# Moving the turns' DRAM transfers and the bias tables from SyncE's queue to GpSimd's in a two-layer encoder

## The chip, the cores and the metric

The kernel runs on one core of a Trainium2 chip. The metric is the device time of one execution in microseconds (us); the kernel before took 889.69 us as the median of three runs (887.34 to 892.37). The engines are TensorE (PE, matrix products; PEld is its weight load), VectorE (DVE), ScalarE (ACT), GpSimd (POOL) and SyncE (SP). SyncE computes nothing here; it issues transfers between DRAM and on-chip memory, which run on 16 DMA engines.

## The reference, cut to what matters

Two residual layers over a sequence of 256 tokens of width 2048, then a final RMSNorm. All data is float32.

```python
def _layer_ab(x, ln, w_in, sink, w_out):
    hn = _rmsnorm(x, ln)
    aq, ak, av, bq, bk, bv, z = jnp.split(hn @ w_in, AB_SPLITS, axis=-1)
    ya = banded attention, 8 heads, 2 key heads, +-128 tokens, ALiBi, a sink per head
    yb = dilated mixture, 8 heads, ALiBi
    y = jnp.concatenate([ya, yb], axis=-1) * jax.nn.silu(z)
    return x + y @ w_out

def _layer_c(x, ln, w_in, rpb, w_out):
    hn = _rmsnorm(x, ln)
    cq, ck, cv, z = jnp.split(hn @ w_in, 4, axis=-1)
    y = neighbourhood attention, 16 heads, learned bias rpb
    return x + (y * jax.nn.silu(z)) @ w_out

def reference(...):
    x = _layer_ab(x, ...); x = _layer_c(x, ...)
    return _rmsnorm(x, ln_f)
```

## The kernel before

Each float32 operand is split into a high part and a rest, both of a type that TensorE multiplies at full rate, and each product is three matmuls (high x high, high x rest, rest x high). All weights come as 296 units of 128 x 1024 float32 (512 KB). One unit goes this way: SyncE loads it into one of five buffers `raw` (L136), ScalarE casts it to `wh` (L149), VectorE subtracts to `wl` (L150); `wh` and `wl` have three buffers each. TensorE then takes 12 matmuls of 512 columns for the unit (L205), or 24 of mixed sizes where a block makes one head (L172, L174).

`plan()` lists the blocks: the projections for values (`v`, `va`), keys (`ka`, `k`, in layer C `k4`), queries (`q`, `q4`), gates (`z`, four in each layer, 8 units each), then the output projections (`o`, `last`). In the text, layer A is the part with the first eight heads, layer B that with the second eight, layer C the second layer with 16 heads. Beside the blocks run the heads: scores on TensorE (L367 to L369), softmax on VectorE and ScalarE (L371 to L388), then a turn of the probabilities, their split (L407, L408) and the product with the values (L161 to L163). A counter of blocks (`tick`, `later`) says in which block each step of a head is written down; steps of gates stand in a list of chores that is worked off by one per unit.

A **turn** transposes a 256 x 256 tile. VectorE transposes 32 x 32 squares (L249), one transfer writes the tile to a DRAM buffer `bounce` (L251), and four transfers read it back, 32 partitions each (L258), into `pT`. A gate makes two turns. In layer C, queries and keys are turned as well, through DRAM buffers `pair` into `ka`. Each head also loads a table of biases, two transfers in layers A and B (L498), one in layer C (L503).

A gate's evacuation is four steps on ScalarE (L464, L465, for each half of the tokens) with steps of VectorE behind them (L466, then L249); it can start when TensorE has finished the block.

Every transfer before stands in SyncE's queue, in one order with the weight loads. Each engine works its instructions in order, and the order is not that of the source alone: when the program is built, a scheduler places the instructions of every engine by its own estimates of when their inputs are there. A change of queue can thus move instructions on other engines. The names end in numbers in the rows of that order (`wh_7434`), which are the same in both programs.

Of the kernel before, what the change touches and what calls it, by code (L numbers as in the profile page):

```python
# [25 lines left out]
B = 32  # L26
# [77 lines left out]
def build(tc, ctx, xt, xr_in, wt, head, sink, rpb, tabs, gl_in, out):  # L104
    nc = tc.nc
# [115 lines left out]
    def to_features(j):  # L221


        cols = [slice(c, c + S) for c in range(j * WO, (j + 1) * WO, S)]
        got = []

        def out_():
            got.extend(turn([xr[:, t, c] for t in range(NT)]) for c in cols)

        def in_():  # L230
            got[:] = [turned(b) for b in got]

        def parts_(i):
            src = got[i].rearrange("p a (c t i) -> p c t a i", c=NT, t=NT)
            for c in range(NT):
                k = cols[i].start // P + c
                h, lo = (xx[:, k, e].rearrange("p (t a i) -> p t a i", t=NT, a=NB) for e in range(2))
                nc.scalar.activation(h, src[:, c], AF.Copy, scale=g[:, 1, k:k + 1])
                for t in range(NT):
                    nc.vector.scalar_tensor_tensor(lo[:, t], src[:, c, t], g[:, 1, k:k + 1], h[:, t].bitcast(F32),  # L240
                                                   op0=OP.mult, op1=OP.subtract)

        return [out_, lambda: None, in_, lambda: None, lambda: parts_(0), lambda: parts_(1)]

    def turn(srcs, nm="bounce", n=3):

        tt = work.tile([P, NB, NT, NT, B], F32, name="tt")
        for t in range(NT):
            nc.vector.transpose(tt[:, :, :, t, :].rearrange("p b c i -> p c b i"), srcs[t])  # L249
        bounce = dram.tile([P, NB, NT * NT * B], F32, name=nm, bufs=n)  # L250
        nc.sync.dma_start(bounce, tt.rearrange("p b c t i -> p b (c t i)"))  # L251
        return bounce

    def turned(bounce, pool=work, nm="pT"):
        pT = pool.tile([P, NB, NT * NT * B], F32, name=nm)
        src = bounce.rearrange("(a j) b x -> b j a x", a=NB)
        for b in range(NB):
            nc.sync.dma_start(pT[b * B:(b + 1) * B], src[b])  # L258
        return pT

    R = {}
# [129 lines left out]
    def transposes(hh, p, v):  # L391

        bounce = turn([p[:, t, :] for t in range(NT)])
        later(1, lambda: back(hh, bounce, v))

    def back(hh, bounce, v):
        pT = turned(bounce)
        later(L2, lambda: parts(hh, pT, v))
# [58 lines left out]
    def gate(pss, j):  # L457
# [13 lines left out]
        def out_(i):  # L471
            got[i] = turn([zr[:, i * S:(i + 1) * S] for zr in zs])

        def in_(i):
            got[i] = turned(got[i])
# [17 lines left out]
    def table_ab(hh):  # L493
        tab = work.tile([P, NT, S], F32, name="tab", bufs=2)
        n = 2 * S - 1
        for t in range(NT):
            src = bass.AP(tensor=tabs.tensor, offset=tabs.offset + hh * n + t * P, ap=[[1, P], [1, S]])
            nc.sync.dma_start(tab[:, t, :], src)  # L498
        return tab

    def table_c(hh):
        tab = work.tile([P, NT, S], F32, name="tab", bufs=2)
        nc.sync.dma_start(tab, rpb[hh])  # L503
        return tab

    def load_x(k0, k1):
# [36 lines left out]
    def start_head(lag, idx, q):  # L543
        if idx < AQ:
            k, v, sc = KA[idx // 4], (lambda: V["a"], idx // 4), (nsk[:, idx:idx + 1], sk[:, idx:idx + 1])
        else:
            vb = V["b"]
            k, v, sc = cur["k"], (lambda: vb, idx % 4), None
        tab = table_ab(idx)
        later(lag, lambda: scores(idx, q, k, v, tab, sc, -1))  # L550
# [16 lines left out]
    def start_pair(lag, j, i, bq, bk):  # L567

        got, tabs_ = {}, []

        def in_():
            for nm, b in (("k", bk), ("q", bq)):
                got[nm] = turned(b[i], qk, "ka")
            tabs_.append(table_c(j))

        def parts_():
            for nm in "kq":
                src = got[nm].rearrange("p a (c t i) -> p c t a i", c=NT, t=NT)
                got[nm] = []
                for c in range(NT):  # L580
                    h = qk.tile([P, S], F32R, name=nm + "h", bufs=3 if nm == "q" else 2)
                    lo = qk.tile([P, S], F32R, name=nm + "l", bufs=3 if nm == "q" else 2)
                    hv, lv = (e.rearrange("p (t a i) -> p t a i", t=NT, a=NB) for e in (h, lo))
                    nc.scalar.copy(hv, src[:, c])
                    nc.vector.tensor_sub(lv, src[:, c], hv.bitcast(F32))
                    got[nm].append((h, lo))

        def score(i):
            v = (lambda: V[j // 4], j % 4 + i)
            scores(j + i, got["q"][i], got["k"][i], v, tabs_[i], None, 1)  # L590

        later(lag, in_)
        later(lag + 1, parts_)
        later(lag + 2, lambda: score(0))
        later(lag + 3, lambda: tabs_.append(table_c(j + 1)))
        later(lag + 2 + PACE, lambda: score(1))
# [132 lines left out]
```

## Time and profile before

| | before |
|---|---|
| median of three runs | 889.69 us |
| profiled execution, time | 889.07 us |
| profiled execution, span | 887.3 us |
| TensorE busy | 868.3 us (98%) |
| VectorE busy | 599.0 us (68%) |
| ScalarE busy | 502.4 us (57%) |
| GpSimd busy | 0.9 us |
| SyncE's DMA queue, share of 16 engines | 71.7% |

Busy time leaves out the issue of transfers, so SyncE has no row here. Matmuls overlap in the records: one of 512 columns shows a span of 0.39 us, and the next starts 0.227 us after it.

### The profile page before, as it was taken

The page shows a single profiled execution, that of the slowest core. Times are in us where ns is not written, and L with a number is a line of the kernel's source. Part 1 is how long each engine was busy: PE and PEld are TensorE (multiplying, and loading weights), DVE is VectorE, ACT ScalarE, POOL GpSimd, SP SyncE. Part 2 cuts the span into 40 slices and gives each one's busy share as a digit, 9 for nine tenths or more (in the row PEclk, how much of TensorE's full clock was granted, in tenths as well). Part 3 has the DMA queues.
Part 4 walks back from the last instruction along what each step waited for, and adds up shares of the span by engine and source line. Part 5 has one row for each costly group of instructions (what it writes and reads, how often), then busy time and mean ns, then how long its engine had stood idle before and what let it go on. Part 6 is the DMA issues. An engine that isn't in the chain of part 4 may idle for free.

```text
span 887.3 us, 12303 instructions
## 1 busy us (share of the span) xinstructions
PE 868.3 (98%) x4218; PEld 732.9 (83%) x4218; DVE 599.0 (68%) x972; ACT 502.4 (57%) x858; POOL 0.9 (0%) x7
## 2 busy tenths in 40 slices
PE   9999999999999999999999999999999998899995
PEld 7898888889888888888888888888888876688884
DVE  6576867788677766667556666766666666666563
ACT  7646666676556555555455565556555655454452
POOL 0000000000000000000000000000000000000000
PEclk9999999999999999999999999999999999999999
DMA  9868777779767677777677767786687578667642
GB/s 353 305 201 256 223 248 254 214 228 278 225 211 233 230 239 252 245 240 241 214 238 233 258 223 259 226 268 243 200 272 272 196 220 297 197 208 274 210 165 96
DMA packets 104607, 209.53 MB, mean 236 GB/s; under 512 B 11744, under 2 KB 52704, under 8 KB 104416
## 3 DMA queue, kind: packets, MB, share of 16 engines
q1 hardware_dynamic: 104544, 208.74, 71.7%
q8 instruction: 33, 0.54, 0.3%
q14 instruction: 30, 0.25, 0.1%
HBM read 187.72 MB, written 20.97 MB: 235 GB/s over the span
## 4 chain that ended last, share of the span: by engine, by line
PE 94%; ACT 2%; DVE 1%; DMA 1%; issue 1%; SPq 0%; ACTq 0%; DVEq 0%
PE pp L205 70%; PE pp L172 10%; PE pp L174 6%; PE pp L293 1%; PE pp L292 1%; PE pp L294 1%; PE pS L369 1%; PE pY L163 1%; PE pY L162 1%; PE pS L368 1%; PE pS L367 1%; PE pY L161 1%; DMA raw<-wt 1%; DMA y<-xt 1%; PE pp L176 1%; ACT wh L149 1%
## 5 line engine op out<-in xcount | busy, mean ns | idle before, releaser
L150 DVE TENSOR_TENSOR wl<-raw,wh 128x1024 fp32r<-128x1024 f32 x291 | 354.5, 1222 | 218.7 <-ACT wh L149 188.8
L205 PE MATMUL pp<-wh,xx 128*128 128x512 f32 (+1 forms) x1472 | 457.1, 387 | 6.3 <-ACT wh L149 6.0
L149 ACT CAST wh<-raw 128x1024 fp32r<-128x1024 f32 x291 | 305.0, 1052 | 255.2 <-PE pp L205 207.1
L205 PEld LDWEIGHTS pp<-wh,xx 128*128 128x128 f32 x1472 | 275.8, 189 | 62.0 <-ACT wh L149 7.0
L205 PE MATMUL pp<-wl,xx 128*128 128x512 f32 (+1 forms) x736 | 285.3, 388 | 2.7 <-DVE wl L150 2.7
L205 PEld LDWEIGHTS pp<-wl,xx 128*128 128x128 f32 x736 | 139.4, 189 | 31.3 <-DVE wl L150 4.9
L205 PE MATMUL pp<-wh,yy 128*128 128x512 f32 x448 | 138.4, 389 | 0.0
L205 PEld LDWEIGHTS pp<-wh,yy 128*128 128x128 f32 x448 | 84.1, 188 | 17.5
L172 PE MATMUL pp<-xx,wh 128*128 128x512 f32 x390 | 93.7, 392 | 0.0
L205 PE MATMUL pp<-wl,yy 128*128 128x512 f32 x224 | 87.1, 389 | 0.0
L172 PEld LDWEIGHTS pp<-xx,wh 128*128 128x128 f32 x390 | 72.1, 188 | 14.6
L174 PEld LDWEIGHTS pp<-xx,wl 128*128 128x128 f32 x416 | 53.3, 191 | 2.0
L174 PE MATMUL pp<-xx,wl 128*128 128x256 f32 x416 | 54.0, 283 | 0.0
L205 PEld LDWEIGHTS pp<-wl,yy 128*128 128x128 f32 x224 | 42.1, 188 | 8.6
L379 ACT ACTIVATE s<-s,nm 128x256 f32<-128x256 f32 x64 | 32.0, 501 | 12.1 <-DVE nm L374 10.2
L371 DVE SCALAR_TENSOR_TENSOR s<-pS,qs,tab 128x256 f32<-128x256 f32 x64 | 28.4, 475 | 5.1 <-PE pS L369 5.0
L249 DVE STREAM_TRANSPOSE tt<-p 128x256 f32<-128x256 f32 x64 | 26.2, 435 | 7.9 <-ACT p L388 7.9
L388 ACT ACTIVATE p<-s,rd 128x256 f32<-128x256 f32 x64 | 29.0, 501 | 4.3 <-DVE rd L385 4.2
L181 ACT COPY sum<-pp 128x256 f32<-128x256 f32 x26 | 9.6, 371 | 37.5 <-PE pp L176 37.4
L407 ACT CAST ph<-pT 128x256 fp32r<-128x256 f32 x64 | 23.3, 405 | 11.3 <-DMA pT<-bounce 11.3
L408 DVE TENSOR_TENSOR pl<-pT,ph 128x256 fp32r<-128x256 f32 x64 | 24.4, 418 | 6.1 <-ACT ph L407 6.0
L374 DVE TENSOR_REDUCE nm<-s 128x2 f32<-128x512 f32 x32 | 21.7, 679 | 0.2
(124 smaller groups left out, 582.5 us busy)
## 6 DMA issues: line engine op xcount, KB each, us to landing
raw<-wt SPq DMA_DIRECT2D x295, 512.0 KB, 4.5
bounce<-tt SPq DMA_DIRECT2D x56, 256.0 KB, 2.7
pT<-bounce SPq DMA_DIRECT2D x224, 64.0 KB, 3.3
tab<-tabs SPq DMA_DIRECT2D x32, 128.0 KB, 4.9
tab<-rpb SPq DMA_DIRECT2D x16, 256.0 KB, 4.1
pair<-tt SPq DMA_DIRECT2D x16, 256.0 KB, 3.0
ka<-pair SPq DMA_DIRECT2D x64, 64.0 KB, 4.0
xr<-xr SPq DMA_DIRECT2D x4, 512.0 KB, 5.2
```

Of the source, the lines that this page charges most:

```text
L149: nc.scalar.copy(h, raw)
L150: nc.vector.tensor_sub(lo, raw, h.bitcast(F32))
L172: nc.tensor.matmul(ps, parts[u][0][:, c], aa[:, k], start=k == 0, stop=False)
L174: nc.tensor.matmul(ps[:, 0], parts[u][1][:, c], aa[:, k, 0], start=False, stop=False)
L205: nc.tensor.matmul(pss[t], aa[:, k, i // 2, t * P:(t + 1) * P], (h, lo, h)[i][:, c], start=k == 0 and i == 0, stop=k == NK - 1 and i == 2)
L249: nc.vector.transpose(tt[:, :, :, t, :].rearrange("p b c i -> p c b i"), srcs[t])
L371: nc.vector.scalar_tensor_tensor(s[:, t, :], pS[:, t, :], R["qs"][:, t:t + 1], tab[:, t, :], op0=OP.mult, op1=OP.add)
L374: nc.vector.tensor_reduce(nm, s, axis=AX.X, op=OP.max, negate=True)
L379: nc.scalar.activation(s[:, t, :], s[:, t, :], AF.Exp, bias=nm[:, t:t + 1], accum_out=den[:, t:t + 1])
L388: nc.scalar.activation(p[:, t, ::step], s[:, t, :], AF.Copy, scale=rd[:, t:t + 1])
L407: nc.scalar.copy(dh, src)
L408: nc.vector.tensor_sub(dl, src, dh.bitcast(F32))
```

## The change

Four places are edited, and in each `nc.sync` becomes `nc.gpsimd`: the write of a turn, its four reads, and the two kinds of bias table. The loads of weights, of the input and of the residual, and the output, stay in SyncE's queue.

```diff
@@ turn
-        nc.sync.dma_start(bounce, tt.rearrange("p b c t i -> p b (c t i)"))
+        nc.gpsimd.dma_start(bounce, tt.rearrange("p b c t i -> p b (c t i)"))
@@ turned
         for b in range(NB):
-            nc.sync.dma_start(pT[b * B:(b + 1) * B], src[b])
+            nc.gpsimd.dma_start(pT[b * B:(b + 1) * B], src[b])
@@ table_ab
-            nc.sync.dma_start(tab[:, t, :], src)
+            nc.gpsimd.dma_start(tab[:, t, :], src)
@@ table_c
-        nc.sync.dma_start(tab, rpb[hh])
+        nc.gpsimd.dma_start(tab, rpb[hh])
```

SyncE, at the first two gates of layer C, before: `raw` are weight loads, `ka` and `pT` reads of turns, `bounce` writes.

```order
L136 DMA raw_7104<-wt 128x1024
L136 DMA raw_7122<-wt 128x1024
L258 DMA ka_7163<-pair_6722 32x4x128 x4
L258 DMA ka_7168<-pair_6495 32x4x128
L251 DMA bounce_7161<-tt_7158 128x512
L258 DMA ka_7168<-pair_6495 32x4x128 x3
L503 DMA tab_7173<-rpb 128x512
L136 DMA raw_7177<-wt 128x1024
L251 DMA bounce_7186<-tt_7183 128x512
L136 DMA raw_7200<-wt 128x1024
```

SyncE at the same place after:

```order
L136 DMA raw_7104<-wt 128x1024
L136 DMA raw_7122<-wt 128x1024
L136 DMA raw_7177<-wt 128x1024
L136 DMA raw_7200<-wt 128x1024
L136 DMA raw_7244<-wt 128x1024
```

Only weight loads are left. GpSimd's queue at this place after:

```order
L251 DMA bounce_7161<-tt_7158 128x512
L251 DMA bounce_7186<-tt_7183 128x512
L258 DMA pT_7223<-bounce_7161 32x4x128 x2
L251 DMA bounce_7209<-tt_7206 128x512
L258 DMA pT_7223<-bounce_7161 32x4x128 x2
L258 DMA pT_7250<-bounce_7186 32x4x128 x4
L258 DMA pT_7273<-bounce_7209 32x4x128 x4
L251 DMA bounce_7375<-tt_7372 128x512
L258 DMA pT_7425<-bounce_7375 32x4x128 x4
```

Writes and reads of turns follow one another there in one order, as they did on SyncE, without weight loads between them.

ScalarE at the end of the second gate of layer C (`pp_7175` and `pp_7176` hold the block), before. `wh_7399` is the last unit of this block, `wh_7434` the first of the next:

```order
L149 CAST wh_7399<-raw_7267 128x1024
L454 CAST yy_88<-y_87 128x256 x2
L464 ACTIVATE s_7415<-pp_7175,rh_4422 128x512
L465 ACTIVATE sq_7416<-pp_7175,rh_4422 128x512
L464 ACTIVATE s_7420<-pp_7176,rh_4422 128x512
L465 ACTIVATE sq_7421<-pp_7176,rh_4422 128x512
L149 CAST wh_7434<-raw_7316 128x1024
L149 CAST wh_7457<-raw_7340 128x1024
```

ScalarE at the same place after:

```order
L149 CAST wh_7399<-raw_7267 128x1024
L379 ACTIVATE s_7297,den_7308<-s_7297,nm_7306 128x256 x2
L454 CAST yy_88<-y_87 128x256 x2
L388 ACTIVATE p_7313<-s_7297,rd_7311 128x256 x2
L454 CAST yy_88<-y_87 128x256
L423 COPY y_87<-pY_7364 128x256
L454 CAST yy_88<-y_87 128x256
L149 CAST wh_7434<-raw_7316 128x1024
L149 CAST wh_7457<-raw_7340 128x1024
L464 ACTIVATE s_7415<-pp_7175,rh_4422 128x512
L465 ACTIVATE sq_7416<-pp_7175,rh_4422 128x512
L464 ACTIVATE s_7420<-pp_7176,rh_4422 128x512
```

The casts of the next block's first two units have moved from behind the gate's evacuation to before it. VectorE's subtractions for these units move in the same way, and so does the third gate of layer C (`pp_7430`). At the other six gates two casts of the next block stand before the evacuation in both programs.

## Rows read from the trace of the kernel before

**Rows 1.** The page: busy time of the engines, chain that ended last.

```profile
PE 868.3 (98%) x4218; PEld 732.9 (83%) x4218; DVE 599.0 (68%) x972; ACT 502.4 (57%) x858; POOL 0.9 (0%) x7
...
PE 94%; ACT 2%; DVE 1%; DMA 1%; issue 1%; SPq 0%; ACTq 0%; DVEq 0%
```

**Rows 2.** TensorE by stretch (from:to, length, busy, count, granted clock, DMA share, GB/s).

```profile
60.00:700.00 640.00, 640.00 (x3155) 1.00 0.74 240
700.00:740.00 40.00, 35.02 (x161) 1.00 0.67 222
740.00:775.00 35.00, 31.36 (x129) 0.90 0.69 225
```

**Rows 3.** Timeline of TensorE, 725 to 790 us: start, length, operation, [idle before <-releaser].

```profile
737.58 0.73 PE L205 MATMUL pp<-wh,xx 128*128 128x512 f32 x2 [2.77 <-ACT wh L149]
739.16 0.50 PE L205 MATMUL pp<-wl,xx 128*128 128x512 f32 x1 [0.85 <-DVE wl L150]
...
765.88 0.73 PE L205 MATMUL pp<-wh,xx 128*128 128x512 f32 x2 [2.77 <-ACT wh L149]
767.48 0.80 PE L205 MATMUL pp<-wl,xx 128*128 128x512 f32 x1 [0.87 <-DVE wl L150]
```

**Rows 4.** TensorE in short stretches behind the two pairs, columns as in rows 2.

```profile
740.00:744.00 4.00, 4.00 (x12) 0.57 0.99 330
768.00:772.00 4.00, 4.00 (x13) 0.66 0.79 243
```

**Rows 5.** Timeline of ScalarE around the second and the fourth gate's evacuation.

```profile
734.17 0.69 ACT L464 ACTIVATE s<-pp,rh 128x512 f32<-128x512 f32 x1 [0.87 <-PE pp L205]
...
736.47 2.95 ACT L149 CAST wh<-raw 128x1024 fp32r<-128x1024 f32 x3
...
788.72 1.05 ACT L149 CAST wh<-raw 128x1024 fp32r<-128x1024 f32 x1 [0.51 <-ACT wh L149]
790.71 0.69 ACT L464 ACTIVATE s<-pp,rh 128x512 f32<-128x512 f32 x1 [0.94 <-PE pp L205]
```

**Rows 6.** SyncE's issues from 695 us, its longest wait there, ScalarE's wait behind it.

```profile
699.02 2.32 SPq L258 DMA_DIRECT2D ka<-pair  x5
...
712.60 0.38 SPq L136 DMA_DIRECT2D raw<-wt  x1
...
SPq L251 <- DVE tt L249: 7.4, 1, 7.4
...
717.18 1.05 ACT L149 CAST wh<-raw 128x1024 fp32r<-128x1024 f32 x1 [2.89 <-DMA raw<-wt]
```

**Rows 7.** DMA issues (count, KB, us to landing); SyncE's time per issue, ns min/median/max.

```profile
bounce<-tt SPq DMA_DIRECT2D x56, 256.0 KB, 2.7
pT<-bounce SPq DMA_DIRECT2D x224, 64.0 KB, 3.3
...
L258 SPq DMA_DIRECT2D pT<-bounce x224: 302/424/1863, 73.4 to 802.1; - x112
L251 SPq DMA_DIRECT2D bounce<-tt x56: 319/327/456, 70.7 to 795.5; - x56
```

**Rows 8.** The page's groups: the transposes of a turn (busy us, mean ns | idle before).

```profile
L249 DVE STREAM_TRANSPOSE tt<-p 128x256 f32<-128x256 f32 x64 | 26.2, 435 | 7.9 <-ACT p L388 7.9
```

**Rows 9.** Chain in order of time (start, length): the periods of layers A and C.

```profile
69.62 16.35 PE pp L205 x72
...
105.51 16.35 PE pp L205 x72
...
488.37 5.47 PE pp L205 x24
...
506.17 5.47 PE pp L205 x24
```

**Rows 10.** ScalarE's waits from 60 to 310 us: total, times, longest.

```profile
ACT ph L407 <- DMA pT<-bounce: 9.9, 4, 3.4
```

**Rows 11.** VectorE's costliest group, columns as in rows 8.

```profile
L150 DVE TENSOR_TENSOR wl<-raw,wh 128x1024 fp32r<-128x1024 f32 x291 | 354.5, 1222 | 218.7 <-ACT wh L149 188.8 <-issue 8.7 <-PE pp L174 6.1
```

## The prediction, made before the changed kernel ran

> **What bounds the kernel now.** I read the page's busy times and chain first. TensorE is busy for 868.3 of 887.3 us, and matmuls make up 94% of the chain that ended last [rows 1]. VectorE, ScalarE and the DMA engines have room. A change can thus only win what TensorE loses, so the next view is its busy time by stretch [rows 2]: nothing lost in the 640 us from 60 to 700, 4.98 us (40 - 35.02) from 700 to 740, 3.64 us (35 - 31.36) from 740 to 775. The rest lies at the head and the tail, which the change doesn't reach. The timeline of TensorE [rows 3] shows where in that stretch: two pairs of gaps, 2.77 + 0.85 us at 737 and 2.77 + 0.87 us at 765, together **7.26 us**; the other 1.4 us are four gaps under 0.5 us from 714 to 732. After each pair the granted clock falls, though TensorE is busy again: over 4 us it averages 0.57 after the first and 0.66 after the second [rows 4], a stretch at the lower of its two levels (1.2 GHz) and the rest at the upper (2.4 GHz). What that costs is the share not granted: 4 x 0.43 + 4 x 0.34 = **3.1 us**.
>
> Why there? The rows of ScalarE [rows 5] show it. At 734.17 ScalarE starts a gate's evacuation (L464), which had to wait until TensorE finished the gate's block, and only behind the four evacuation steps comes the next cast of weights, at 736.47; VectorE's half follows. TensorE has nothing split in advance, so it stands still. The third gate's pair at 765 has the same releasers and sizes [rows 3]. At the fourth gate, casts (the last at 788.72) stand ahead of the evacuation at 790.71, and TensorE has no gap there. It is an order on two engines, fixed when the program is built: I counted the weight units cast ahead of each gate's evacuation beyond that gate's own block. Of the eight gates six have two units ahead, and the second and third gate of layer C have none.
>
> SyncE's queue shows the rest [rows 6]: from 699.02 to 712.60 no weight load is issued, because a turn's write (L251) waits 7.4 us for its transposes and the loads stand behind it. ScalarE then waits for weights, 2.89 us before 717.18, and the four small gaps lie about and after that.
>
> **What the change does, step by step.** It moves 408 transfers from SyncE to GpSimd, counted in the order of the changed program: 72 writes (56 to `bounce`, 16 to `pair`), 288 reads back (four for each) and 48 bias tables. SyncE loses 72 x 0.33 + 288 x 0.42 = 145 us of issuing [rows 7], and the tables'; it is not on the path, so that alone is worth nothing. What counts is what stood behind them: weight loads now wait only for one of their five buffers. The 13.6 us hole can't recur, and I take the 1.4 us of small gaps as gone.
>
> The larger part comes with the build. The order of the changed program has two units of the next block ahead of all eight gates, on ScalarE and on VectorE alike, the two bad ones included (wh_7434 and wh_7457 now stand before the evacuation of pp_7175). That is the place of the six good gates, and TensorE lost nothing at those. So both pairs go, with the clock after them: 7.26 + 3.1 = **10.3 us** (10.34).
>
> Against this stands a longer turn. GpSimd's price p of a transfer isn't in this trace; it is busy for 0.9 us in all [rows 1]. Bounds from the nearest rows: SyncE's issue of the same transfers, 0.33 to 0.42 us, below, and the longest that any of them took there, 1.86 us, above [rows 7]. Below the lower bound nothing would change, since even at SyncE's price the sum doesn't hang on p. I take 0.4 to 1.2 us, nearer the medians than the one longest row, and work out where p begins to matter.
>
> *Latency.* A turn writes (2.7 us to landing), then issues four reads in a row, the last landing 3.3 us after its issue [rows 7]: 2.7 + (p - 0.33) + 3p + 3.3 + (p - 0.42) = 5.25 + 5p, which is 7.4 us at SyncE's price. In the changed order the tightest turns have three weight units between transposes and first use (15 of the 56 turns that pass through `bounce`; 28 have four, 13 five). In layer C a unit takes 17.8 / 6 = 2.97 us [rows 9]. ScalarE casts unit k when TensorE frees the buffer of unit k-3, so transposes end 1.05 (a cast, [rows 5]) + 1.22 (a subtraction, [rows 11]) + 2 x 0.435 [rows 8] = 3.1 us after one such point, and the first use stands 1.05 us after a point three units later: 3 x 2.97 + 1.05 - 3.1 = 6.8 us are free. Beyond that ScalarE waits, and TensorE's split units cover 3 x 2.97 - 1.05 - 0.87 - 2.27 = 4.7 us of it (the cast before, two casts of pT, taken like the transposes of that tile, and cast and subtraction of the next unit). That such waits are covered the trace shows: from 60 to 310 us ScalarE waits up to 3.4 us for pT [rows 10], and TensorE is never idle there [rows 2]. So a turn costs nothing until 5.25 + 5p exceeds 6.8 + 4.7 = 11.5, **p = 1.25**.
>
> *Throughput.* A waiting transfer holds all behind it on GpSimd, so each write-to-read wait (2.7 us) counts as use. Layer A, per gate and two heads: 24 transfers and three waits in 35.9 us [rows 9], full at p = 27.8 / 24 = 1.16. Layer B, per head: 7 and one in four units, 11.9 us at C's pace, 1.31. Layer C, per head: 11 and one in 17.8 us, 1.37. The second gate of C: 21 and two in about 24 us (96 matmuls at 16.35 / 72 = 0.227 us are 21.8, and heads), 0.89; there a backlog of 21p + 5.4 - 24 forms, 3.6 us at p = 1.06, which the cover above absorbs. So up to p near 1.2 the sum is the same.
>
> The page "DMA: Bandwidth & Descriptors" of the Trainium skill (section "Latency and other measured facts") gives about 0.6 us to the first byte from SyncE's kind of queue and about 1 us from GpSimd's. By that, as an estimate, p would be 0.42 + 0.4 = 0.8 us and the sum unchanged; no run here shows it yet.
>
> At the start one table load now stands on GpSimd ahead of its copy of the gains (L532); that copy has to wait for the first input transfer, and the load lies beside this wait.
>
> **Sum.** 889.07 - 10.3 = 878.8; the 1.4 us of small gaps go, and I put the same amount back for turns that come late at the crowded second gate. The profiled execution lies 0.6 us below the median of the three runs; I say **879.0 us**, 1.2% faster.
>
> **Rivals.** *GpSimd's queue becomes the bound.* From about p = 1.25 on it is slower. At p = 1.3 layer A is over by 24 x 1.3 + 8.1 - 35.9 = 3.4 us, three times; C's second gate by 8.7, the two gates after it by 15 x 1.3 + 5.4 - 24 = 0.9 each; late turns add some 1: 878.8 + 22 = 901 us. What could make p so large is VectorE holding up the writing of descriptors. Its rows [rows 11] are 291 subtractions with two operands in SBUF of 1.22 us, 354.5 us of busy time; were a transfer held for one of them, p would be 0.43 + 1.22 = 1.65 and the time 878.8 + 131 = 1010 us (A 35, B 19, C 49, gates 28). Against it: such a subtraction is under way 40% of the time, so a transfer would wait 0.4 x 0.6 = 0.25 us on average, p = 0.7. The page "SBUF — State Buffer" of the Trainium skill (section "Who interferes with whom") speaks against this change: the writing of GpSimd's transfers starves while VectorE runs in a mode that takes both ports, which copies and tensor_scalar can enter but tensor_tensor has no such mode. By that rule these subtractions leave it alone, and the sum stands.
>
> *The gaps are paid back.* Weight loads start as soon as a buffer is free and meet the turns on the same 16 engines; in stretches these are already full (share 0.99 from 740 to 744) [rows 4]. With p around 1.2 and landings of 4 to 8 us instead of 3.3, the 15 tight turns leave TensorE short by 0.5 us each, with a dip of the clock: 878.8 + 10 = 889 us, no change. For it: that DMA share. Against: 640 us at a mean share of 0.74 without a gap [rows 2].
>
> *The change doesn't do what it says.* Were lateness of weights not behind anything, the time would stay at 889. But six good gates against two bad ones speak for the order, which the build has changed.
>
> **How the numbers follow.** Forecast (876 to 885 us) 0.65; paid back or without effect (885 to 894) 0.14; GpSimd as the bound (894 to 1010) 0.21. Half a per cent, 4.4 us, is about what a measurement of this kernel can tell from no change, so these are also the chances of faster, same and slower. The low end, 876 us, has the 1.4 us gone as well and 1 us of noise; to leave out no more than 2 in 10, the high end goes to p = 1.28, 898 us.
>
> **What would show it.** Right: no gap over 0.5 us on TensorE from 730 to 775, clock 1.00 there, no ScalarE wait for raw, about 878 us; ScalarE's waits for pT longer than 3.4 us in places, with TensorE busy. Right on p: GpSimd's transfers start 0.4 to 1.2 us apart. Wrong: starts over 1.25 us apart with reads queued behind reads, ScalarE waiting for pT at most heads, TensorE idle from about 70 us on (layer A first), the clock at 0.50 again and again.

## The result, and the profile after

| | before | after |
|---|---|---|
| median | 889.34 us | **940.11 us** (936.38 to 946.85) |
| ratio | | 1.058, 95% interval 1.053 to 1.062 |
| profiled execution, span | 887.3 us | 937.4 us |
| mean granted clock of TensorE | 0.994 | 0.982 |
| TensorE idle before its last matmul, in gaps over 0.1 us | 10.0 us, 10 gaps | 41.6 us, 37 gaps |

The changed kernel is 5.8% slower. The medians in this table come from runs side by side on one chip. The forecast was 879 us and the range ended at 898, so the time lies far outside it. (The gaps were added up from the timeline of TensorE; the first of each column is the 1.05 us ahead of the first matmul.) The median before is over six executions, one of which took 4205 us; without it the median is 888.99 us.

The page of the changed kernel: busy times, as in [rows 1], and its DMA issues (count, KB each, median us from issue to landing), as in [rows 7].

```profile
PE 887.5 (95%) x4218; PEld 739.3 (79%) x4218; DVE 595.3 (64%) x972; ACT 498.6 (53%) x858; POOL 224.4 (24%) x415
...
raw<-wt SPq DMA_DIRECT2D x295, 512.0 KB, 4.4
bounce<-tt POOLq DMA_DIRECT2D x56, 256.0 KB, 3.2
pT<-bounce POOLq DMA_DIRECT2D x224, 64.0 KB, 4.7
```

Reads that took 3.3 us to land now take 4.7; writes take 3.2 instead of 2.7. GpSimd is busy for a quarter of the span, so issuing doesn't fill its time.

The waits of the changed kernel (engine, line, what it waited for: total us, times, longest us):

```profile
ACT wh L149 <- PE pp L205: 144.9, 92, 3.8
ACT ph L407 <- DMA pT<-bounce: 133.1, 30, 8.8
...
DVE pl L408 <- ACT ph L407: 106.0, 27, 8.0
...
PE pp L205 <- ACT wh L149: 18.3, 10, 3.5
...
PE pp L205 <- DVE wl L150: 14.0, 16, 2.1
```

The second row is the new one. Before, ScalarE waited for `pT` 7 times, 11.3 us in all and 3.4 at most; now it waits 30 times, 133.1 us in all and up to 8.8. ScalarE works in order, so the next casts of weights stand behind such a wait, and the last two rows are TensorE's waits for those casts and for VectorE's half.

TensorE by stretch, columns as in [rows 2] with every engine's count:

```profile
60.00:700.00 640.00, 612.91 (x2964) 512.20 (x2964) 413.01 (x681) 342.02 (x603) 171.47 (x313) 0.99 0.71 224
700.00:740.00 40.00, 35.09 (x156) 28.19 (x155) 23.70 (x38) 21.57 (x40) 16.28 (x30) 0.96 0.77 235
740.00:775.00 35.00, 35.00 (x167) 29.41 (x166) 22.34 (x34) 18.71 (x32) 9.45 (x18) 1.00 0.69 229
```

From 60 to 700 us, where TensorE lost nothing before [rows 2], it is now idle for 640 - 612.9 = 27.1 us. In the changed kernel's stretch from 740 to 775 it is full.

One of the turns, 318 to 338 us. The timelines of the engines (start, length, engine, line, operation, [idle before <-releaser]), merged by start:

```profile
318.16 0.41 ACT L407 CAST ph<-pT 128x256 fp32r<-128x256 f32 x1 [4.46 <-DMA pT<-bounce]
...
320.86 1.05 ACT L149 CAST wh<-raw 128x1024 fp32r<-128x1024 f32 x1
...
320.96 16.67 SPq L136 DMA_DIRECT2D raw<-wt  x5
...
321.82 0.42 DVE L249 STREAM_TRANSPOSE tt<-p 128x256 f32<-128x256 f32 x1
...
322.24 1.05 ACT L149 CAST wh<-raw 128x1024 fp32r<-128x1024 f32 x1
...
322.54 0.56 POOL L251 DMA_DIRECT2D bounce<-tt  x1 [8.20 <-DVE tt L249]
...
323.80 1.05 ACT L149 CAST wh<-raw 128x1024 fp32r<-128x1024 f32 x1 [0.50 <-PE pp L205]
...
326.74 2.19 POOL L258 DMA_DIRECT2D pT<-bounce  x4 [3.64 <-issue]
...
332.55 0.41 ACT L407 CAST ph<-pT 128x256 fp32r<-128x256 f32 x1 [7.43 <-DMA pT<-bounce]
...
336.08 0.49 PE L205 MATMUL pp<-wh,xx 128*128 128x512 f32 x1 [2.69 <-ACT wh L149]
337.34 0.79 PE L205 MATMUL pp<-wl,xx 128*128 128x512 f32 x1 [0.77 <-DVE wl L150]
```

The first row is the end of the previous turn's wait. This turn's transposes end at 322.24, its write goes out at 322.54, the four reads from 326.74 to 328.93, and ScalarE can go on at 332.55, 10.0 us after the write. It waited 7.43 us; TensorE lived on its split units for 4.0 of them and then stood still for 2.69 + 0.77 us. All the while SyncE issued weight loads, five from 320.96 on. In the kernel before, at the next turn of the same part of the program, SyncE's own timeline reads:

```profile
305.73 0.33 SPq L251 DMA_DIRECT2D bounce<-tt  x1
307.46 0.33 SPq L136 DMA_DIRECT2D raw<-wt  x1
307.88 1.80 SPq L258 DMA_DIRECT2D pT<-bounce  x4
309.78 7.24 SPq L136 DMA_DIRECT2D raw<-wt  x4
```

One weight load goes out between write and reads, and the next four only after the reads.

### The profile page after: what moved, and what is told of

Same layout as the page of the kernel before. It is cut to its first block, busy times and chain, and to the rows that moved or that the text cites. A ratio compares the mean times of both kernels' runs of the same rounds, so it can differ in the third digit from the quotient of the medians.

```text
span 937.4 us, 12426 instructions
## 1 busy us (share of the span) xinstructions
PE 887.5 (95%) x4218; PEld 739.3 (79%) x4218; DVE 595.3 (64%) x972; ACT 498.6 (53%) x858; POOL 224.4 (24%) x415
## 5 line engine op out<-in xcount | busy, mean ns | idle before, releaser
L205 PE MATMUL pp<-wh,xx 128*128 128x512 f32 (+1 forms) x1472 | 466.1, 393 | 20.2 <-ACT wh L149 17.6
L149 ACT CAST wh<-raw 128x1024 fp32r<-128x1024 f32 x291 | 300.9, 1049 | 161.2 <-PE pp L205 144.9
L205 PEld LDWEIGHTS pp<-wh,xx 128*128 128x128 f32 x1472 | 280.4, 192 | 80.9 <-ACT wh L149 21.6
L205 PE MATMUL pp<-wl,xx 128*128 128x512 f32 (+1 forms) x736 | 290.6, 395 | 13.3 <-DVE wl L150 13.3
L205 PEld LDWEIGHTS pp<-wl,xx 128*128 128x128 f32 x736 | 141.4, 192 | 46.0 <-DVE wl L150 19.4
L258 POOL DMA_DIRECT2D pT<-bounce x224 | 122.4, 554 | 131.9 <-DMA bounce<-tt 69.7
L407 ACT CAST ph<-pT 128x256 fp32r<-128x256 f32 x64 | 23.3, 404 | 133.1 <-DMA pT<-bounce 133.1
L251 POOL DMA_DIRECT2D bounce<-tt x56 | 31.2, 558 | 242.2 <-DVE tt L249 231.1
L172 PEld LDWEIGHTS pp<-xx,wh 128*128 128x128 f32 x390 | 72.1, 188 | 14.8 <-ACT wh L149 0.4
L498 POOL DMA_DIRECT2D tab<-tabs x32 | 17.6, 555 | 104.4 <-DVE s L371 103.9
L258 POOL DMA_DIRECT2D ka<-pair x64 | 34.9, 551 | 30.3 <-DMA pair<-tt 13.1
```

What stands on the lines that cost most here:

```text
L149: nc.scalar.copy(h, raw)
L172: nc.tensor.matmul(ps, parts[u][0][:, c], aa[:, k], start=k == 0, stop=False)
L205: nc.tensor.matmul(pss[t], aa[:, k, i // 2, t * P:(t + 1) * P], (h, lo, h)[i][:, c], start=k == 0 and i == 0, stop=k == NK - 1 and i == 2)
L251: nc.gpsimd.dma_start(bounce, tt.rearrange("p b c t i -> p b (c t i)"))
L258: nc.gpsimd.dma_start(pT[b * B:(b + 1) * B], src[b])
L407: nc.scalar.copy(dh, src)
```

## The experiments

Two theories. **Theory 1:** transfers that GpSimd issues are slow by themselves (their landing, or GpSimd's price for each). **Theory 2:** whose queue it is doesn't matter; what matters is that weights and turns stood in one queue. There the waits for transposes and for a write's landing held the weight loads back too, so a turn's reads met few of them on the DMA engines. In two queues the weights run on beside the turns. Two side causes were open too: the tighter order that the build made, and the tables at the start. (The texts on record call the second theory Rival 2 in the swap and Theory 2 from the light weights on; under later use, Theory 1 means late turns in a tight order.)

All the runs in one table. "In flight" is the mean number of weight loads issued and not landed when a read is issued; "turn" runs from the write's issue to the landing of the last of its four reads, median and 95th percentile over the 56 turns through `bounce`. Both were worked out from the traces' transfers. "Wait" is ScalarE's row for `pT` at L407 (L413 in the light kernel).

| kernel | queue of weights / writes / reads / tables | in flight | read lands, us | turn, us | wait, us | time, us | ratio to before, 95% |
|---|---|---|---|---|---|---|---|
| before | SP / SP / SP / SP | 1.27 | 3.3 | 8.1, 11.5 | 11.3 | 889 | 1 |
| after | SP / POOL / POOL / POOL | 1.79 | 4.7 | 10.7, 13.6 | 133.1 | 940.1 | 1.053 to 1.062 |
| e1_swap | POOL / SP / SP / SP | 1.78 | 5.2 | 10.8 | 139.1 | 942.4 | 1.055 to 1.063 |
| e2_later_use | as after | 1.84 | 4.7 | 11.5 | 57.1 | 914.2 | 1.024 to 1.032 |
| e3_turns_only | SP / POOL / POOL / SP | 1.80 | 4.7 | 11.1 | 127.6 | 938.8 | 1.053 to 1.058 |
| e4_tables_only | SP / SP / SP / POOL | 1.08 | 2.9 | 7.4 | 19.4 | 880.6 | 0.988 to 0.991 |
| e5_light_weights | as after, loads of 64 KB | 1.00 | 2.3 | 7.1 | 14.8 | 876.7 | 0.984 to 0.989 |
| e6_writes_only | SP / POOL / SP / SP | 0.80 | 2.7 | 7.4 | 13.4 | **876.1** | 0.984 to 0.987 |
| e7_reads_only | SP / SP / POOL / SP | 1.87 | 4.7 | 11.4 | 144.4 | 932.9 | 1.045 to 1.058 |
| e8_tables_writes | SP / POOL / SP / POOL | 0.77 | 2.3 | 7.4 | 20.7 | 877.9 | 0.986 to 0.991 |
| e9_all_gpsimd | POOL / POOL / POOL / POOL | 1.12 | 2.8 | 8.5, 12.9 | 12.6 | 899.2 | 1.009 to 1.012 |
| e10_reads_weights | POOL / SP / POOL / POOL | 0.65 | 2.2 | 9.3, 12.4 | 46.7 | 892.1 | 1.001 to 1.004 |

**The swap.** The kernel before, with the weights on GpSimd and all the rest left on SyncE.

```diff
-            nc.sync.dma_start(raw, wt[pos[0]])
+            nc.gpsimd.dma_start(raw, wt[pos[0]])
```

> The other way round: the 295 weight loads go through GpSimd's queue, all turns and tables stay in SyncE's, so there are again two queues and no weight load stands behind a turn. Its built order is as tight as that of the change (19 turns with three units between transposes and first use, 25 with four, 12 with five; the change 15, 28, 13), with two units ahead of all eight gates. Theory 1 (a transfer that GpSimd issues lands later by itself: reads 4.7 us against 3.3, a whole turn 10.7 against 8.1): turns are issued by SyncE again, so reads land in at most 3.3 us, ScalarE's waits for pT fall from 133 us to under 40, TensorE's gaps go, 878 to 884 us; weights landing a little later are covered by five buffers. Rival 2 (two queues share the DMA engines, so each turn gets a part of them beside the weights): reads land in 4.7 us again, 925 to 945 us. Rival 3 (the tighter built order alone): 915 to 945 us with reads at 3.3 us.

Measured: 942.37 us. Its page's issues and its wait:

```profile
raw<-wt POOLq DMA_DIRECT2D x295, 512.0 KB, 4.7
bounce<-tt SPq DMA_DIRECT2D x56, 256.0 KB, 3.8
pT<-bounce SPq DMA_DIRECT2D x224, 64.0 KB, 5.2
...
ACT ph L407 <- DMA pT<-bounce: 139.1, 28, 8.5
```

The reads stand in SyncE's queue as they did before, and land even later than in the changed kernel. Theory 1 falls: the loss comes with the separation, whichever side GpSimd gets. Not all of the 942 us is the turns', though: in the first 60 us TensorE is busy for 48.94 us, against 58.58 before, by a slow start that the last two kernels below show too.

**Later use.** The changed kernel with what was turned used two steps of the program's counter later (L2 stands in `later(L2, ...)`).

```diff
-L2 = 1
+L2 = 3
```

> The change, with the split of a turned tile written down two blocks later (lag 3 instead of 1). In the built order 3 turns have three units before first use, 14 four, 24 five, 15 six or more (the change: 15, 28, 13, none), so about one unit, 3 us, more on average. Theory 1 (turns take 10.7 us and the order leaves 6.8 to 9.8): the wait of ScalarE for pT falls from 133 us to about 30 to 50, two thirds of the loss goes, 895 to 910 us. Rival 4 (GpSimd's queue or the DMA engines lack throughput): a later use only shifts the wait, 930 to 945 us.

Measured: 914.16 us. Only 3 of the 56 turns now have three units between transposes and first use (15 in the changed kernel, 4 in the one before), and the wait falls from 133.1 to 57.1 us. But reads still take 4.7 us, and it is 2.8% slower than before. The text gave 895 to 910 us and a wait of 30 to 50. So the tight order decides how much of the late landing gets through, about half; it isn't what makes turns late. The two go together in the other runs: counted in the built order, the kernels with reads in another queue than weights of full size have 15 to 19 turns with three units (changed, swap, turns alone, reads alone), those with both in one queue 2 to 5. Only this run and the light weights take them apart.

**Turns alone, tables alone.** Of the changed kernel the tables put back on SyncE (L498, L503); and of the kernel before only these two lines on GpSimd.

```diff
-            nc.gpsimd.dma_start(tab[:, t, :], src)
+            nc.sync.dma_start(tab[:, t, :], src)
...
-        nc.gpsimd.dma_start(tab, rpb[hh])
+        nc.sync.dma_start(tab, rpb[hh])
```

> Only the turns in GpSimd's queue, the 48 bias tables back in SyncE's. Theory 1: nearly all of the loss stays, but for the first gap of TensorE (2.47 us at 10.9 us, with the lower clock behind it, together some 4 us), which the early tables on GpSimd cause by filling the DMA engines when the input is loaded: 930 to 938 us, first gap 0.4 us as before. Rival (the tables hold up the turns in GpSimd's queue): under 915 us.

> Only the 48 bias tables in GpSimd's queue, turns and weights in SyncE's. Theory 1: no turn is slower; the early tables cost some 4 us at the start (gap of about 2.5 us near 10.9 us), and the built order has two units ahead of six gates and one ahead of the last two of layer C, so some of the 10 us there comes back: 882 to 892 us. Rival (tables are the cause): over 915 us.

Measured: 938.77 us and 880.60 us, 0.8 us above and 1.4 us below what the texts gave. The loss is the turns'; the tables alone make the kernel about 1% faster. What they cost stands at the start. TensorE's first gap of over 1 us, from the timeline of tables alone:

```profile
10.56 0.51 PE L205 MATMUL pp<-wh,xx 128*128 128x512 f32 x1 [2.34 <-ACT xx L156]
```

The changed kernel has one of 2.46 us there, turns alone none over 0.36 us. With GpSimd's queue idle at the start, the tables of the first heads go out at once and run beside the first input (its loads `y<-xt` land after 11.1 us in the changed kernel, 7.6 before). Between the changed kernel and turns alone this makes 1.3 us, which their intervals don't separate.

**Light weights.** The changed kernel, each weight load cut to an eighth and used eight times over, so that every engine's work and order stay. It leaves out seven eighths of the weights, so its output isn't the model's.

```diff
-            raw = wp.tile([P, UNIT], F32, name="raw", bufs=AHEAD)
-            nc.sync.dma_start(raw, wt[pos[0]])
+            raw = wp.tile([P, LIGHT], F32, name="raw", bufs=AHEAD)
+            nc.sync.dma_start(raw, wt[pos[0]][:, :LIGHT])
```

> The change with an eighth of the weight traffic: each weight load moves 64 KB instead of 512 KB and its 128 columns are used eight times, so the products are not the model's; every instruction on the engines, both queues and the built order (15 turns with three units, 28 with four, 13 with five) stay those of the change. Theory 2 (after the swapped queues: a turn whose transfers run in another queue than the weights shares the DMA engines with them, while in one queue the weights had to stand behind): with little to share, reads land in about 2.5 us instead of 4.7, a turn takes about 8 us instead of 10.7, ScalarE's wait for pT falls from 133 us to under 20, 874 to 884 us. Theory 1 (GpSimd's transfers are slow by themselves): reads stay at 4.5 us or more, 930 to 940 us. Rival 3 (the built order alone): turns get faster, and the time stays over 915 us.

Measured: 876.65 us. Its issues, its wait, and TensorE from 60 to 700 and from 700 to 780 us:

```profile
raw<-wt SPq DMA_DIRECT2D x295, 64.0 KB, 1.9
bounce<-tt POOLq DMA_DIRECT2D x56, 256.0 KB, 2.3
pT<-bounce POOLq DMA_DIRECT2D x224, 64.0 KB, 2.3
```

```profile
60.00:700.00 640.00, 640.00 (x3154) 543.01 (x3153) 446.10 (x727) 372.95 (x653) 191.34 (x348) 1.00 0.31 85
700.00:780.00 80.00, 80.00 (x374) 66.98 (x373) 59.48 (x97) 49.57 (x85) 25.25 (x46) 1.00 0.31 98
```

Same queues, same order, same number of transfers on GpSimd; only the bytes of the weights are fewer (the last two columns: DMA share 0.31, 85 and 98 GB/s). TensorE then loses nothing in 720 us. GpSimd's queue and the built order are harmless as such; the loss needs the weights' bytes on the DMA engines.

**Writes alone, reads alone.** Of the kernel before one line each.

```diff
-        nc.sync.dma_start(bounce, tt.rearrange("p b c t i -> p b (c t i)"))
+        nc.gpsimd.dma_start(bounce, tt.rearrange("p b c t i -> p b (c t i)"))
```

```diff
-            nc.sync.dma_start(pT[b * B:(b + 1) * B], src[b])
+            nc.gpsimd.dma_start(pT[b * B:(b + 1) * B], src[b])
```

> Only the 72 writes of the turns in GpSimd's queue; reads and tables in SyncE's with the weights. Built order: 5 turns with three units, 39 four, 10 five, 2 six; all gates with two units ahead. Theory 2: SyncE waits for the landing of each write before it issues the reads, and the weights behind them wait too, so the reads find the DMA engines less busy, landing in about 3.0 us; 876 to 888 us. Theory 1: writes land at 3.3 instead of 2.75 us, reads at 3.3, a turn 8.6 us, 880 to 892 us. The two part on the next run.

> Only the 288 reads of the turns in GpSimd's queue; writes and tables in SyncE's with the weights. Built order: 17 turns with three units, 29 four, 10 five. Theory 2: the reads run beside weights that no longer wait for them and land in 4.5 us or more, the writes still hold the weights while they wait for their transposes; 905 to 940 us. If the writes alone were what the change slowed: under 895 us.

Measured: 876.12 us and 932.87 us. From the waits of the first and of the second:

```profile
ACT ph L407 <- DMA pT<-bounce: 13.4, 8, 3.0
```

```profile
ACT ph L407 <- DMA pT<-bounce: 144.4, 29, 8.3
```

The reads are what must not stand apart from the weights. With the writes alone on GpSimd, SyncE's queue still halts the weights until each write has landed, and the reads go out into emptier DMA engines (0.80 loads in flight, landing 2.7 us). The weights no longer wait for transposes, and the build places two units ahead of all eight gates, as in the changed kernel. TensorE, in the first of these two:

```profile
60.00:700.00 640.00, 640.00 (x3153) 543.09 (x3152) 444.07 (x723) 371.25 (x650) 33.11 (x61) 1.00 0.74 241
700.00:780.00 80.00, 78.55 (x366) 65.43 (x366) 59.33 (x98) 49.08 (x87) 4.86 (x9) 1.00 0.74 255
```

Both pairs of gaps of [rows 3] are gone and the clock is whole. Of the kernels with the model's output it is the fastest, 1.4% under the kernel before.

**Tables and writes.** Writes on GpSimd, tables too, except those of the first two heads.

```diff
-            nc.sync.dma_start(tab[:, t, :], src)
+            (nc.sync if hh < 2 else nc.gpsimd).dma_start(tab[:, t, :], src)
```

> Tables and writes in GpSimd's queue, reads in SyncE's with the weights, and the tables of the first two heads left in SyncE's, behind the first weights. Theory 2: the reads are covered by the order of SyncE's queue as in the kernel before, all gates have two units ahead, the gap at 10.6 us (2.3 us and 1.7 us of lower clock with tables alone on GpSimd) goes: 874 to 880 us, below the 880.6 us of the tables alone. If the early tables on GpSimd are not what opens that gap, it stays and the time is 880 to 884 us.

Measured: 877.86 us, not to be told apart from writes alone. The start's gap shrinks to 0.23 us, so those first tables made most of it; not all, perhaps, for writes alone has 1.26 us at the same place with every table on SyncE and its input landing after 7.6 us.

**All on GpSimd; reads with the weights on GpSimd.** Two kernels that put Theory 2 at risk. In the first, L136, L251, L258, L498 and L503 all issue on GpSimd; in the second, all of these but L251.

```diff
-            nc.sync.dma_start(raw, wt[pos[0]])
+            nc.gpsimd.dma_start(raw, wt[pos[0]])
...
-            nc.sync.dma_start(pT[b * B:(b + 1) * B], src[b])
+            nc.gpsimd.dma_start(pT[b * B:(b + 1) * B], src[b])
```

> The kernel before with all of these transfers in one queue again, but GpSimd's: weights, writes, reads and bias tables. Built order as loose as before's: at the second and third gates of the 4096-row layer the rotated tile's transposes have no unit ahead. Theory 1 (transfers issued by GpSimd are slow by themselves): reads land at 4.7 us or more, ScalarE's wait for pT is over 100 us, time 925 us or more. Theory 2 (it is the weight loads running freely beside the turns' reads, in a queue of their own, that delays the reads; one queue's own waits hold the weights back): reads land near 3.3 us, ScalarE's wait for pT under 30 us, time 885 to 897 us, near the kernel before.

> The mirror of the run with the writes alone on GpSimd: here the reads, the weights and the tables share GpSimd's queue, and the writes alone stand in SyncE's. Theory 2: what counts is that reads and weights share one queue, whichever it is, so reads land at 2.5 to 3.3 us, ScalarE's wait for pT stays under 30 us, and the time is 874 to 886 us, below the kernel before. Theory 1 (GpSimd's transfers are slow by themselves): reads land at 4.7 us, 925 us or more.

(The "4096-row layer" of the first text is layer C.) Measured: 899.20 us and 892.12 us, 2 and 6 us above what Theory 2 gave (885 to 897, 874 to 886). Issues and waits of the first:

```profile
raw<-wt POOLq DMA_DIRECT2D x295, 512.0 KB, 4.6
bounce<-tt POOLq DMA_DIRECT2D x56, 256.0 KB, 3.1
pT<-bounce POOLq DMA_DIRECT2D x224, 64.0 KB, 2.8
...
ACT ph L407 <- DMA pT<-bounce: 12.6, 8, 3.4
```

and its TensorE by stretch:

```profile
0.00:60.00 60.00, 49.42 (x252) 42.27 (x253) 33.48 (x61) 32.40 (x56) 13.97 (x32) 0.91 0.74 263
60.00:300.00 240.00, 240.00 (x1320) 209.26 (x1320) 177.79 (x308) 148.86 (x285) 110.55 (x204) 1.00 0.73 231
300.00:500.00 200.00, 200.00 (x910) 166.61 (x909) 130.30 (x205) 104.57 (x154) 89.09 (x165) 1.00 0.68 238
```

From the page and the waits of the second:

```profile
bounce<-tt SPq DMA_DIRECT2D x56, 256.0 KB, 4.2
pT<-bounce POOLq DMA_DIRECT2D x224, 64.0 KB, 2.2
...
ACT ph L407 <- DMA pT<-bounce: 46.7, 20, 4.1
```

Put back into one queue, reads land fast; the first kernel's wait is as small as before, and its TensorE loses nothing from 60 to 500 us; the two pairs at the gates are back with the same 2.77 us each. In the second, the writes are what stands apart from the weights, and they take 4.2 us; the wait grows to 46.7 us, more than the 30 expected, but no single one exceeds 4.1 us, inside the cover of 4.7, and TensorE loses under 1 us from 60 to 700. So the mechanism holds on GpSimd's side too. What is too long is the first 60 us: 49.42 us busy (58.58 before) at a clock of 0.91 (1.00 before). VectorE's timeline there:

```profile
17.86 0.17 DVE L609 TENSOR_SCALAR nsk<-sk 128x8 f32<-128x8 f32 x1 [7.36 <-DMA sk<-sink]
```

SyncE, with nothing else in its queue, issues the 4 KB load of `sk` at 5.13 us and four 512 KB loads of `xr` from 7.74 (20.33 and 23.05 before), VectorE waits 7.36 us for the small one, and TensorE has a gap of 6.93 us behind that. The second kernel has the same gap (7.01 us); it has no such pairs at the gates, though one gap of 2.5 us at 727, and comes out 0.1 to 0.4% slower than before. TensorE's busy time in the first 60 us is 58.58 - 49.42 = 9.2 us shorter in the first kernel, nearly the 9.7 us by which it is slower than before, and 8.5 us shorter in the second. That these early loads alone make the start slow was not tried on its own.

## Why the prediction was wrong, point by point

**The step that failed: the latency of a turn, 5.25 + 5p, set against 6.8 us of free time; both terms were off.** The latency first. Its landing times, 2.7 and 3.3 us, were medians of the kernel before [rows 7], and they were carried over to a kernel in which the weights run in a queue of their own. With p = 0.555 they give 8.0 us; the changed kernel's median turn takes 10.7. (The formula was short for the kernel before too: 7.4 us at SyncE's price, 8.1 measured.) The trace of before held the missing price. There, the median read landed after 2.0 us with no weight load in flight at its issue (24 reads), 2.9 with one (116) and 4.9 with two (84); the changed kernel's reads take 2.2, 3.8 and 4.9, and 6.0 with three. What changed most is how many meet which: 138 of 224 meet two loads and 24 three, where 84 met two and none three. In parts, the medians over the 56 turns went from 2.75 us (landing of the write), 0.06 (on to the first read), 1.37 (to the fourth) and 3.09 (landing of the last read) to 3.23, 0.56, 1.65 and 4.95: the landing of the last read grew most.

**The free time.** The allowance of 6.8 + 4.7 = 11.5 us is that of a turn with three units; with 2.97 us for each more unit it is 14.5 for four and 17.4 for five. Of the 56 turns 17 take more than 11.5 us, by 23.2 us in sum, but 16 of these have four or five units: past its own allowance are only two, by 2.9 us. So turns as long as measured, put into the prediction's sum, would still have cost next to nothing. What is left over lies mostly in the 6.8 us. In the light kernel, which has the same order, ScalarE is ready for `pT` 6.7 us after the transposes (median of the 15 tight turns), as the prediction had it; in the changed kernel after 5.5 us, at the least 2.9. With four units, where the same reckoning would give 9.8, it is 8.4 and 7.7 (23 turns that ScalarE uses first). (These times were worked out from the traces and the built order.) The turn shown above is the one of 2.9 us: its transposes end at 322.24, and ScalarE is ready at 332.55 - 7.43 = 325.12. Its rows tell why. The probabilities that it transposes come from ScalarE, and came only behind the previous turn's wait at 318.16; then ScalarE's casts of weights, behind by that wait, start at 320.86, 322.24 and 323.80, 1.4 and 1.6 us apart instead of 2.97, with 0.50 us of waiting for TensorE. So a late turn left less time for the next. That this holds for the other turns is argued from this one and the medians, not shown.

The cover was right: taking TensorE's gaps from the ScalarE wait (for `pT` at L407) that each follows leaves 3.9 to 5.3 us of cover in 8 of 11 cases (4.0 of 7.43 in the turn shown above, 4.6 of 8.82 at the longest wait). In the other three it was 2.0 to 2.8 us; each had another wait 8 to 15 us before it, but so had the turn shown above. Why their cover was smaller stays open.

**The bill.** Against writes alone, which has the same two units ahead at all gates, the changed kernel's span is longer by 937.4 - 874.7 = 62.7 us: gaps 41.6 - 3.9 = 37.7; clock not granted 0.018 x 937.4 - 0.002 x 874.7 = 15.1; the other 9.9 lie in TensorE's busy time and I can't allot them to rows. The lower clock follows the gaps, as [rows 4] showed it; the changed kernel from 255 to 262 us, behind a gap of 2.92 us:

```profile
255.00:262.00 7.00, 6.21 (x15) 4.63 (x16) 4.15 (x5) 3.28 (x6) 0.55 (x1) 0.52 0.56 166
```

**The rival that had the mechanism** was "the gaps are paid back": weight loads start as soon as a buffer is free and meet the turns on the same engines. It was priced at 10 us (15 turns, 0.5 us each, with a dip), because it let turns be late only with p near 1.2, and it had 0.14 together with no effect. Its price is 61 us (940 less 878.8), at p = 0.555. The argument against it, 640 us at a DMA share of 0.74 without a gap, was no argument: that share was reached in an order in which SyncE's waits kept weights and reads apart.

**GpSimd's price** was right: 0.4 to 1.2 us were said, the page gives

```profile
L258 POOL DMA_DIRECT2D pT<-bounce x224 | 122.4, 554 | 131.9 <-DMA bounce<-tt 69.7
```

554 ns each, and with VectorE busy 64% of the time none of the 224 took more than 567 ns, so no subtraction of 1.22 us held one up. So the rival in which GpSimd's queue becomes the bound, and its thresholds of 0.89 to 1.37, never came into play. Two of its signs came all the same, from late turns: ScalarE waits for `pT` at 30 of the 32 heads, and the lower clock comes again and again. The estimate from the Trainium skill, page "DMA: Bandwidth & Descriptors", section "Latency and other measured facts", 0.8 us, was high by 0.25.

**The gates' 10.3 us** were right, and so was reading them from the order: where turns aren't late (writes alone, tables and writes, light weights) the pairs are gone and the time is 876 to 878 us, where the sum said 878.8. The changed kernel has them gone too, but gaps of late turns stand in the same stretch, so 35.09 of 40 us are busy from 700 to 740, as before. Two small slips in the sum: the dips of the clock cost 3.4 us rather than 3.1, for the second began before the stretch in [rows 4] (767 to 771 us: 0.57); and 878.8 with the 0.6 us named there is 879.4, not 879.0.

**The hole in SyncE's queue** was read as a loss only. ScalarE's wait for `raw` did shrink, from 19.7 to 4.7 us in the changed kernel; but the same halts were what kept the DMA engines open for the reads.

**The start** was wrong in kind: GpSimd's copy didn't matter; the early tables' traffic beside the first input did, by most of a gap of 2.46 us.

## What to carry to other kernels

Before a bulk stream and a chain of small, dependent transfers go to different queues, sort the landing times of the small ones by how many bulk loads are in flight at their issue: that list told here what a read costs once the queue's own waits no longer hold the bulk back, though not how often it pays. A wait that blocks a stream with buffers to spare may be doing useful scheduling, so move only what the stream shouldn't wait for (here the writes, whose wait is for transposes) and leave in its queue what must go out ahead of it (the reads). A slack worked out from an undisturbed order holds only while nothing is late: here it shrank with the first late turns, from 6.7 to 5.5 us at the median.

## What the runs showed of the hardware

The change of queue by itself had little effect on a transfer: with few bytes beside them, GpSimd's reads landed after 2.3 us at the median in the light kernel, and SyncE's after 2.0 in the kernel before when no load was in flight. The Trainium skill, page "DMA: Bandwidth & Descriptors", section "Issuing engines are not separate DMA queues", says that transfers started by different engines run on the same 16 DMA engines and interleave, and that using several issuers only saves the time of issuing. The swap agrees with the first half (reads at 5.2 us from SyncE's queue, 4.7 from GpSimd's). The second half is too narrow for this kernel: the issuers also decide which transfers are under way together, and that moved the time from 876 us (writes alone) to 940 us (the change) with the same bytes.

Nor is it the mean load: with mean landing times of 4.72 and 4.74 us, weight loads in flight are on average 295 x 4.72 / 937.4 = 1.5 in the changed kernel and 295 x 4.74 / 887.3 = 1.6 in the one before. Reads met 1.79 in the changed kernel and 1.27 in the one before. So one order kept the reads in the valleys of the weights' traffic and the other set them on its crests; why on the crests, rather than at the mean, wasn't tested.
